# Queries and keys of both layers: one transfer of 128 partitions fills a tile, keys' two parts in one tensor, queries of layer 1 stored by block and map

## The chip, the core and the metric

The kernel runs on one core of one Trainium2 chip. The core has five engines with programs of their own: PE (TensorE, matrix products and transposes), DVE (VectorE), ACT (ScalarE), POOL (GpSimd) and SP (SyncE, which here does nothing but issue transfers). Transfers between the chip's main memory (DRAM) and the on-chip tiles of 128 partitions are carried by 16 DMA engines. SP issues nearly all of them, in the order of its program; a transfer that has to wait for a tile or for data holds up all that stand behind it on SP.

The metric is the device time of one execution in microseconds (us). Durations of single instructions and packets come from one profiled execution.

## What is computed

A trunk of two layers over 2048 tokens of width 1024, in float32. Cut to what matters here:

```python
def even_layer(x, ...):                       # layer 0
    proj = rms_norm(x, norm_g) @ w_in         # queries, keys, values, gates of mixers A and B
    ya = sliding_window_sink_attention(aq, ak, av, a_sinks) * silu(ag)    # 8 query heads, 2 key heads
    yb = chunked_relbias_attention(bq, bk, bv, b_rel) * silu(bg)          # 8 heads
    return x + concatenate([ya, yb]) @ w_out

def odd_layer(x, ...):                        # layer 1
    q, k, v, gate = split(rms_norm(x, norm_g) @ w_in)
    # 8 heads, each with two maps: q1, k1 and q2, k2 of width 64
    a = softmax(q1 @ k1.T / 8) - lam * softmax(q2 @ k2.T / 8)             # keys of the own and earlier chunks
    o = rms_norm(a @ v, subln_g) * (1 - lambda_init)
    return x + (o * silu(gate)) @ w_out
```

## The kernel before

**Two parts of a number.** A product that must be nearly exact is made of two parts of each operand: H, the value rounded to the fast matrix format, and L, the rest. `eH` and `eL` are such a pair for queries and keys. A head has 64 dimensions, which is half of the 128 partitions. A key tile holds H of a head's keys in one half of its partitions and L in the other; a query tile holds the same 64 rows twice, once for each half. So one product over 128 partitions adds query times H and query times L. `qd` holds the H part of the queries twice, `ql` the L part twice.

**Stages.** Four follow each other; a block is 512 tokens, there are four, `b` = 0 to 3.
1. *Projection of layer 0* (`project(0)`): norm, product with the weights, norm and rotation of queries and keys, transposes. `pairs_out` copies each transposed pair of heads into `eH` and `eL` (three buffers each) and stores them to DRAM (L398 and L399), 128 partitions by 512 tokens at a time.
2. *Attention of layer 0* (`mix0`): 16 heads by four blocks, from the last block to the first. `load_q` (L577 to L581) fills `qd` and `ql` (three buffers each) by four transfers of 64 partitions; `load_k` (L587 and L588) fills a key tile by two, H and L. `mks` is the key tile of mixer B (two buffers, 1024 tokens), `mksA` that of mixer A (one for four heads). Output projection and late gates run beside it.
3. *Projection of layer 1* (`project(1)`): two halves of the tokens, in each six groups of weights of 512 columns: values, queries (two groups), keys (two groups), values. Each group is applied to two blocks. Again `pairs_out` stores, in the query groups to `qH` and `qL`, in the key groups to `kH` and `kL`.
4. *Attention of layer 1* (`mix1`): for each head blocks 0 and 1, then block 2 of all heads, then block 3. `load_q` (L926) fills `cqd` and `cql` (two buffers each) by two transfers of 64 partitions each; one row of such a transfer is 2 pieces of 2 KB, one for each map. `load_k` (L1093 and L1094) fills a key tile `ck` of one block and map, H and L apart; there are four buffers for each map. Block `b` needs `b + 1` key tiles for each map; block 3 fills all four buffers, so the next head's keys are loaded as the last row of this head's scores lets go of them. Gates and output projection run beside it.

**What sets the order.** The generators `pace` and `beside` hand out the work of scores, values and side work, and a scheduler then orders each engine's program when the kernel is built.

Queries and keys pass through DRAM: stored by projection, loaded by attention. In DRAM each of `qH`, `qL`, `kH`, `kL` (layer 1), `aqH` ... `bkL` (layer 0) is a tensor of its own, a row of 2048 tokens for each dimension of a head.

Of the kernel before, what the change touches and what calls it, by code (L numbers as in the profile page):

```python
# [11 lines left out]
F32R = mybir.dt.float32r  # L12
# [6 lines left out]
P = 128  # L19
S = 2048  # L20
# [3 lines left out]
BLK = NTB * P  # L24
NB = S // BLK
HD = 64
# [6 lines left out]
def f32(ap):  # L33
    return ap.bitcast(F32)
# [52 lines left out]
class Trunk:  # L87
# [15 lines left out]
    def scratch(self):  # L103
        dram = self.ctx.enter_context(self.tc.tile_pool(name="scr", bufs=1, space=DRAM))

        def d(name, shape):
            return dram.tile(shape, F32, tag=name, name=name)

        self.s0 = {
            "aqH": d("aqH", [4, P, S]), "aqL": d("aqL", [4, P, S]),  # L110
            "akH": d("akH", [1, P, S]), "akL": d("akL", [1, P, S]),
            "av": d("av", [S, 2 * 192]),
            "bqH": d("bqH", [4, P, S]), "bqL": d("bqL", [4, P, S]),
            "bkH": d("bkH", [4, P, S]), "bkL": d("bkL", [4, P, S]),
            "bv": d("bv", [S, 8 * 128]),
            "g": d("g0", [D, S]),
            "woH": d("wo0H", [KT, P, D]), "woL": d("wo0L", [KT, P, D]),
        }
        self.s1 = {
            "qH": d("qH", [8, P, S]), "qL": d("qL", [8, P, S]),  # L120
            "kH": d("kH", [8, P, S]), "kL": d("kL", [8, P, S]),
            "v": d("v", [S, D]),
            "g": d("g1", [D, S]), "o": d("o1", [D, S]),
            "hH": d("hH", [KT, P, S]), "hL": d("hL", [KT, P, S]),
            "woH": d("wo1H", [KT, P, D]), "woL": d("wo1L", [KT, P, D]),
            "wgH": d("wgH", [8, P, KT, P]), "wgL": d("wgL", [8, P, KT, P]),
        }
        self.x1 = d("x1", [S, D])
# [95 lines left out]
    def _project(self, es, layer):  # L224
        nc, tc, a = self.nc, self.tc, self.a
        x = a["x"] if layer == 0 else self.x1
        W = a["ev_w_in"] if layer == 0 else a["od_w_in"]
        s = self.s0 if layer == 0 else self.s1
        n = f"p{layer}"
# [154 lines left out]
        def pairs_out(xs, npair, b, o):  # L384
            for p in range(npair):
                ps = ptr.tile([P, 512], F32, tag="tr", name=n + "trq")
                for j in range(NTB):
                    nc.tensor.transpose(ps[:, j * P:(j + 1) * P], xs[j][:, p * P:(p + 1) * P], self.ident)
                eH = sb.tile([P, 512], F32R, tag="eH", name=n + "eH", bufs=3)
                eL = sb.tile([P, 512], F32R, tag="eL", name=n + "eL", bufs=3)  # L390
                g = self.b_gain
                if not o.get("gain"):
                    nc.scalar.activation(eH, ps, AF.Copy)
                    nc.vector.tensor_tensor(eL, ps, f32(eH), ALU.subtract)
                else:
                    nc.scalar.activation(eH, ps, AF.Copy, scale=g)
                    nc.vector.scalar_tensor_tensor(eL, ps, g, f32(eH), ALU.mult, ALU.subtract)
                nc.sync.dma_start(s[o["dH"]][o["p0"] + p, :, b * BLK:(b + 1) * BLK], f32(eH))  # L398
                nc.sync.dma_start(s[o["dL"]][o["p0"] + p, :, b * BLK:(b + 1) * BLK], f32(eL))  # L399

        def split_weights(W, c0, put, s=s):
            for i in range(2):
# [29 lines left out]
        for half in range(2):  # L432
# [4 lines left out]
            if half == 0 and layer == 0:  # L437
# [3 lines left out]
                h = [hidden(blocks[0], 0, by)]  # L441
            else:
                h = [hidden(blocks[0], 0)]
# [4 lines left out]
            for gi, (kind, c0, width, o) in enumerate(groups):  # L448
# [7 lines left out]
                for bi, b in turns:  # L456
# [21 lines left out]
                    for j in range(NTB):  # L478
                        t = b * NTB + j
                        tok = slice(t * P, (t + 1) * P)  # L480
# [72 lines left out]
    def _mix0(self, es):  # L553
        nc, tc, a, s = self.nc, self.tc, self.a, self.s0
        n = "m"
        pool = lambda nm, bufs, **kw: es.enter_context(tc.tile_pool(name=n + nm, bufs=bufs, **kw))
        sm = pool("sm", 6)
        ld = pool("ld", 2)
# [13 lines left out]
        def load_q(H, L, h, b, res):  # L572
            tok = slice(b * BLK, (b + 1) * BLK)
            e = h % 2
            r = slice(e * HD, (e + 1) * HD)
            qd = ld.tile([P, BLK], F32R, tag="qd", name=n + "qd", bufs=3)
            nc.sync.dma_start(f32(qd[0:HD, :]), s[H][h // 2, r, tok])  # L577
            nc.sync.dma_start(f32(qd[HD:P, :]), s[H][h // 2, r, tok])
            ql = ld.tile([P, BLK], F32R, tag="ql", name=n + "ql", bufs=3)
            nc.sync.dma_start(f32(ql[0:HD, :]), s[L][h // 2, r, tok])  # L580
            nc.sync.dma_start(f32(ql[HD:P, :]), s[L][h // 2, r, tok])  # L581
            res["q"] = (qd, ql)

        def load_k(ks, H, L, p, row, k0, k1):

            r = slice(row * HD, (row + 1) * HD)
            nc.sync.dma_start(f32(ks[0:HD, :k1 - k0]), s[H][p, r, k0:k1])  # L587
            nc.sync.dma_start(f32(ks[HD:P, :k1 - k0]), s[L][p, r, k0:k1])  # L588
            return ks


# [11 lines left out]
        def load_group(b, g):  # L603

            k0, k1 = max(0, b * BLK - P), (b + 1) * BLK
            ks = ld.tile([P, 640], F32R, tag="ksA", name=n + "ksA", bufs=1)
            load_k(ks, "akH", "akL", 0, g, k0, k1)
            vt = ld.tile([P, 5, 192], F32R, tag="vA", name=n + "vA", bufs=1)
            nc.sync.dma_start(
                f32(vt[:, :(k1 - k0) // P, :]),  # L610
                s["av"][k0:k1, g * 192:(g + 1) * 192].rearrange("(t p) c -> p t c", p=P),
            )
            return ks, vt, k0
# [108 lines left out]
        def scores_b(h, b, res):  # L722
            k0, k1 = max(0, (b - 1) * BLK), (b + 1) * BLK
            load_q("bqH", "bqL", h, b, res)
            ks = load_k(ld.tile([P, 1024], F32R, tag="ks", name=n + "ks"), "bkH", "bkL", h // 2, h % 2, k0, k1)
            vt = ld.tile([P, 8, P], F32R, tag="v", name=n + "vB")
            nc.sync.dma_start(
                f32(vt[:, :(k1 - k0) // P, :]),
# [6 lines left out]
            l, r = small("bl", 4), small("br", 4)  # L735
            probs = res["p"] = []
            res.update(v=vt, k0=k0)
            for j in range(NTB):
                t = b * NTB + j
# [5 lines left out]
                m = small("bm", 2)  # L745
# [147 lines left out]
    def _mix1(self, es):  # L893
        nc, tc, a, s = self.nc, self.tc, self.a, self.s1
        n = "c"
        pool = lambda nm, bufs, **kw: es.enter_context(tc.tile_pool(name=n + nm, bufs=bufs, **kw))
        ld = pool("ld", 2)
# [19 lines left out]
            return sm.tile([P, m], F32, tag=tag, name=n + tag)  # L917

        def load_q(h, b):
            tok = slice(b * BLK, (b + 1) * BLK)  # L920
            qd = ld.tile([P, 2, BLK], F32R, tag="qd", name=n + "qd")
            ql = ld.tile([P, 2, BLK], F32R, tag="ql", name=n + "ql")
            for part, q in (("qH", qd), ("qL", ql)):
                both = s[part][h, :, tok].rearrange("(m r) t -> r m t", m=2)
                for o in range(2):
                    nc.sync.dma_start(f32(q[o * HD:(o + 1) * HD]), both)  # L926
            return qd, ql

        def scores(h, b, q, K, res, then):
# [158 lines left out]
        def load_k(h, i, m):  # L1088

            tok = slice(i * BLK, (i + 1) * BLK)  # L1090
            k = kp.tile([P, BLK], F32R, tag=f"k{m}", name=n + f"k{m}")
            r, o = slice(m * HD, (m + 1) * HD), slice((1 - m) * HD, (2 - m) * HD)
            nc.sync.dma_start(f32(k[r, :]), s["kH"][h, r, tok])  # L1093
            self.loaded = nc.sync.dma_start(f32(k[o, :]), s["kL"][h, r, tok]).ins  # L1094
            return k

        def load_v(h, i):
# [266 lines left out]
```

## Time and profile before

| | |
|---|---|
| Time, median of 3 runs (lowest, highest) | 2790.53 us (2790.26, 2792.29) |
| The profiled execution's own time | 2787.34 us |
| Its span, first to last instruction | 2785.4 us |
| PE, DVE, ACT, POOL busy, share of the span | 96%, 65%, 57%, 51% |
| Moved by DMA | 521.64 MB, 187 GB/s on average |
| Stages, by the first and last products of each | layer 0: projection to 560, attention to 1168; layer 1: projection to 1734, attention to the end |

How to read what follows. The page has the busy time of each engine, the DMA queues and the chain of work that ended last. A view by windows gives busy times, the share of time in which the 16 DMA engines are busy, and GB/s for each stretch. A list of DMA issues has one row for each kind of transfer: where to and from, who issued it, how many, KB each, and the median time in us from issue to landing. The view of one tile lists its instructions (count: least, median, greatest duration in ns) and what ended the idle time before them. "DMA x<-y" is a transfer into tile x.

### The profile page before, as it was taken

To read this page: it belongs to the slowest core of one execution; us is meant where nothing else is said; L and a number is where in the kernel's file an instruction comes from. 1 tells how busy PE (TensorE), PEld (TensorE's weight loads), DVE (VectorE), ACT (ScalarE), POOL (GpSimd) and SP (SyncE) were. 2 spreads that over 40 slices of the span, in tenths; PEclk is the share of its full clock that TensorE was granted. 3 is DMA by queue.
4 is the path that set the end of the run, shared out by engine and by line. 5 is a ranking of instruction groups with operands and counts; after the bars stand their busy time and mean duration, and the time that the engine had idled before them with its cause. 6 is when DMAs were issued, how large, how long until landed. Compare 5 with 4: busy or idle time off the path is not lost.

```text
span 2785.4 us, 43642 instructions
## 1 busy us (share of the span) xinstructions
PE 2687.8 (96%) x13384; PEld 2164.0 (78%) x13384; DVE 1814.8 (65%) x4520; ACT 1596.8 (57%) x3975; POOL 1425.9 (51%) x1519
## 2 busy tenths in 40 slices
PE   7999999999899999999999999999999999999999
PEld 6888887888788888788888888777777776676776
DVE  8662286336678776457844783478887787776772
ACT  5443544357777776333243332588887776676771
POOL 3641255235545454325554552467776666667661
PEclk9999999999999999999999999999999999999999
DMA  5674338739777665654386446899877666455542
GB/s 184 213 240 149 110 129 275 239 116 248 221 200 202 192 188 154 200 212 142 130 269 222 131 134 194 250 247 249 213 219 207 198 182 195 125 176 150 165 130 91
DMA packets 354041, 521.64 MB, mean 187 GB/s; under 512 B 42768, under 2 KB 137744, under 8 KB 353808
## 3 DMA queue, kind: packets, MB, share of 16 engines
q1 hardware_dynamic: 349200, 510.47, 61.0%
q10 hardware_dynamic: 4608, 8.39, 0.8%
q8 instruction: 107, 1.75, 0.3%
q14 instruction: 126, 1.03, 0.1%
HBM read 361.70 MB, written 157.02 MB: 186 GB/s over the span
## 4 chain that ended last, share of the span: by engine, by line
PE 68%; DMA 6%; DVE 3%; ACT 3%; issue 2%; POOL 1%; SPq 1%; ACTq 0%; DVEq 0%; POOLq 0%
PE cO L1010 8%; PE p1mm L216 6%; PE p1mm L215 6%; PE p1mm L214 6%; PE cS L951 4%; PE cS L952 4%; PE ctr L1006 4%; PE mom L214 2%; PE mom L215 2%; PE mom L216 2%; PE com L214 2%; PE cG L214 2%; PE com L215 2%; PE cG L215 2%; PE com L216 2%; PE cG L216 2%
## 5 line engine op out<-in xcount | busy, mean ns | idle before, releaser
L958 ACT ACTIVATE cP<-cS,cnm 128x512 f32<-128x512 f32 (+3 forms) x640 | 394.6, 623 | 137.9 <-DVE cnm L955 126.4
L955 DVE TENSOR_REDUCE cnm<-cS 128x1 f32<-128x512 f32 (+3 forms) x640 | 373.4, 600 | 53.8 <-PE cS L952 47.6
L992 POOL TENSOR_TENSOR cP<-cP,cP 128x512 f32<-128x512 f32 (+1 forms) x320 | 356.2, 1140 | 19.2 <-ACT cP L990 18.6
L991 POOL TENSOR_SCALAR cP<-cP,crl,cel 128x512 f32<-128x512 f32 (+3 forms) x288 | 208.8, 737 | 258.4 <-DVE crl L973 111.8
L216 PE MATMUL p1mm<-p1wH,p1hL 128*128 128x512 f32 x768 | 300.5, 392 | 0.0
L214 PE MATMUL p1mm<-p1wH,p1hH 128*128 128x512 f32 x768 | 300.2, 393 | 0.0
L215 PE MATMUL p1mm<-p1wL,p1hH 128*128 128x512 f32 x768 | 299.4, 390 | 0.0
L309 POOL TENSOR_TENSOR p0wL<-p0ws,p0wH 128x512 fp32r<-128x512 f32 (+1 forms) x140 | 169.9, 1240 | 251.0 <-ACT p0wH L307 232.4
L1010 PE MATMUL cO<-cpt,cv 128*128 128x512 f32 (+3 forms) x640 | 286.9, 534 | 5.6 <-DVE cpt L1008 5.6
L951 PE MATMUL cS<-ck,cqd 128*128 128x512 f32 (+3 forms) x640 | 260.6, 411 | 12.5 <-ACT cP L958 11.1
L1008 DVE COPY cpt<-ctr 128x512 f32<-128x512 f32 (+1 forms) x320 | 190.6, 604 | 101.0 <-PE ctr L1006 98.1
L214 PE MATMUL p0mm<-p0wH,p0hH 128*128 128x512 f32 (+1 forms) x640 | 239.1, 377 | 7.4 <-ACT p0vt L497 5.4
L216 PE MATMUL p0mm<-p0wH,p0hL 128*128 128x512 f32 (+1 forms) x640 | 239.3, 374 | 1.3 <-DVE p0hL L335 1.3
L215 PE MATMUL p0mm<-p0wL,p0hH 128*128 128x512 f32 (+1 forms) x640 | 239.5, 374 | 0.0
L952 PE MATMUL cS<-ck,cql 128*128 128x512 f32 (+3 forms) x640 | 233.1, 369 | 1.7 <-DMA cql<-qL 1.7
L1006 PEld LDWEIGHTS ctr<-ident,cP 128*128 128x128 f32 x1088 | 137.3, 141 | 120.0 <-issue 62.6
L309 POOL TENSOR_TENSOR p1wL<-p1ws,p1wH 128x512 fp32r<-128x512 f32 x112 | 154.3, 1402 | 138.8 <-ACT p1wH L307 80.6
L990 ACT ACTIVATE cP<-cP,cc 128x512 f32<-128x512 f32 (+1 forms) x320 | 188.9, 653 | 20.6 <-DVE cc L976 19.6
L1006 PE MATMUL ctr<-ident,cP 128*128 128x128 f32 x1088 | 174.8, 274 | 5.7 <-POOL cP L992 5.7
L216 PEld LDWEIGHTS p1mm<-p1wH,p1hL 128*128 128x128 f32 x768 | 144.2, 188 | 29.4
L215 PEld LDWEIGHTS p1mm<-p1wL,p1hH 128*128 128x128 f32 x768 | 144.3, 188 | 29.0
L214 PEld LDWEIGHTS p1mm<-p1wH,p1hH 128*128 128x128 f32 x768 | 144.3, 188 | 28.5
(320 smaller groups left out, 6937.3 us busy)
## 6 DMA issues: line engine op xcount, KB each, us to landing
p1ws<-in_od_w_in_dram SPq DMA_DIRECT2D x56, 512.0 KB, 3.7
p0ws<-in_ev_w_in_dram SPq DMA_DIRECT2D x48, 512.0 KB, 4.5
ck<-kH SPq DMA_DIRECT2D x144, 128.0 KB, 3.6
ck<-kL SPq DMA_DIRECT2D x144, 128.0 KB, 3.8
cv<-v SPq DMA_DIRECT2D x72, 256.0 KB, 4.4
cqd<-qH SPq DMA_DIRECT2D x64, 256.0 KB, 6.2
cql<-qL SPq DMA_DIRECT2D x64, 256.0 KB, 7.6
cwH<-wgH SPq DMA_DIRECT2D x64, 256.0 KB, 5.3
```

The costliest lines, as they stand in the source:

```text
L214: mm(ps, aH, bH, start=first, stop=False)
L215: mm(ps, aH, bL, start=False, stop=False)
L216: mm(ps, aL, bH, start=False, stop=last)
L309: low.tensor_tensor(l[:, :width], ws[:, k, :width], f32(h[:, :width]), ALU.subtract)
L951: mm(ps, qd[:, m, js], kt[:, :wd], start=True, stop=False)
L952: self.anchor = mm(ps, ql[:, m, js], kt[:, :wd], start=False, stop=True).ins
L955: nc.vector.tensor_reduce(nm[:, m, z:z + 1], ps, AX.X, ALU.max, negate=True)
L958: exp = nc.scalar.activation(chunks[z][:, :wd], ps, AF.Exp, bias=nm[:, m, z:z + 1], accum_out=acc).ins
L991: nc.gpsimd.tensor_scalar(p1, p1, rl[:, 0:1], e1, ALU.mult, ALU.mult)
L992: nc.gpsimd.tensor_tensor(p1, p1, p2, ALU.add)
L1006: nc.tensor.transpose(turned[:, (j - j0) * P:(j - j0 + 1) * P], us[j][kt // 4][:, kk:kk + P], self.ident)
L1010: mm(O[:, j0 * P:], v, T[:, :wd], start=(kt == 0), stop=(kt == nkt - 1), skip_group_check=True)
```

## The change

- The keys' H and L parts become one tensor: `ak`, `bk` and `ck` have a dimension of 2 for the parts. The names `akH`, `akL` and so on remain as views of it for the stores.
- A key load becomes one transfer. Its source is a pattern of 2 parts by 64 dimensions by the tokens; its destination is 128 partitions by the tokens. In layer 1, H now always lies in the lower 64 partitions; before, this depended on the map. The query tile has the same rows in both halves, so the product is the same sum.
- A query load becomes one transfer for each of `qd` and `ql`. Its source is the 64 rows with a leading dimension of 2 and a step of zero, so that each row is read twice; its destination is 128 partitions.
- Queries of layer 1 are stored as `[head, 64, block, map, 512]`: the two maps of a block lie side by side, and a row of a query load is one piece of 4 KB. The store of a pair (128 partitions, two maps of 64) now goes to a pattern of 2 by 64 by 512.

```diff
+        ak, bk, ck = d("ak", [1, 2, P, S]), d("bk", [4, 2, P, S]), d("ck", [8, 2, P, S])
...
-            "akH": d("akH", [1, P, S]), "akL": d("akL", [1, P, S]),
+            "ak": ak, "akH": ak[:, 0], "akL": ak[:, 1],
...
-            "bkH": d("bkH", [4, P, S]), "bkL": d("bkL", [4, P, S]),
+            "bk": bk, "bkH": bk[:, 0], "bkL": bk[:, 1],
...
-            "qH": d("qH", [8, P, S]), "qL": d("qL", [8, P, S]),
-            "kH": d("kH", [8, P, S]), "kL": d("kL", [8, P, S]),
+            "qH": d("qH", [8, HD, NB, 2, BLK]), "qL": d("qL", [8, HD, NB, 2, BLK]),
+            "k": ck, "kH": ck[:, 0], "kL": ck[:, 1],
...
-                nc.sync.dma_start(s[o["dH"]][o["p0"] + p, :, b * BLK:(b + 1) * BLK], f32(eH))
-                nc.sync.dma_start(s[o["dL"]][o["p0"] + p, :, b * BLK:(b + 1) * BLK], f32(eL))
+                for part, t in (o["dH"], eH), (o["dL"], eL):
+                    to = s[part][o["p0"] + p]
+                    by_map = layer == 1 and o["tab"] == "q"
+                    to = to[:, b].rearrange("r m t -> m r t") if by_map else to[:, b * BLK:(b + 1) * BLK]
+                    nc.sync.dma_start(to, f32(t))
...
-            nc.sync.dma_start(f32(qd[0:HD, :]), s[H][h // 2, r, tok])
-            nc.sync.dma_start(f32(qd[HD:P, :]), s[H][h // 2, r, tok])
...
-            nc.sync.dma_start(f32(ql[0:HD, :]), s[L][h // 2, r, tok])
-            nc.sync.dma_start(f32(ql[HD:P, :]), s[L][h // 2, r, tok])
+            for q, part in (qd, H), (ql, L):
+                nc.sync.dma_start(f32(q), s[part][h // 2, r, tok].unsqueeze(0).to_broadcast([2, HD, BLK]))
...
-            nc.sync.dma_start(f32(ks[0:HD, :k1 - k0]), s[H][p, r, k0:k1])
-            nc.sync.dma_start(f32(ks[HD:P, :k1 - k0]), s[L][p, r, k0:k1])
+            nc.sync.dma_start(f32(ks[:, :k1 - k0]), s[K][p, :, r, k0:k1])
...
-                both = s[part][h, :, tok].rearrange("(m r) t -> r m t", m=2)
-                for o in range(2):
-                    nc.sync.dma_start(f32(q[o * HD:(o + 1) * HD]), both)
+                both = s[part][h, :, b].rearrange("r m t -> r (m t)")
+                nc.sync.dma_start(f32(q).rearrange("p m t -> p (m t)"), both.unsqueeze(0).to_broadcast([2, HD, 2 * BLK]))
...
-            r, o = slice(m * HD, (m + 1) * HD), slice((1 - m) * HD, (2 - m) * HD)
-            nc.sync.dma_start(f32(k[r, :]), s["kH"][h, r, tok])
-            self.loaded = nc.sync.dma_start(f32(k[o, :]), s["kL"][h, r, tok]).ins
+            self.loaded = nc.sync.dma_start(f32(k), s["k"][h, :, m * HD:(m + 1) * HD, tok]).ins
```

The next rows are SP's program, where the kernel's transfers stand in the order of issue: line, destination and source, and the destination's pattern, outermost dimension first. First, attention of layer 0, the loads for one head of mixer A and one of mixer B (`mvB` and `mbias` are values and bias of mixer B). Before:

```order
L577 DMA mqd<-aqH 64x512
L578 DMA mqd<-aqH 64x512
L580 DMA mql<-aqL 64x512
L727 DMA mvB<-bv 128x8x128
L581 DMA mql<-aqL 64x512
L587 DMA mks<-bkH 64x1024
L588 DMA mks<-bkL 64x1024
L732 DMA mbias<-in_relb_dram 128x256
```

The same place with the change:

```order
L584 DMA mqd<-aqH 128x1x512
L584 DMA mql<-aqL 128x1x512
L590 DMA mks<-bk 128x1x1024
L729 DMA mvB<-bv 128x8x128
L734 DMA mbias<-in_relb_dram 128x256
```

Six transfers of 64 partitions have become three of 128. The destination has been given a dimension of 1, so that it has as many dimensions as the source, which is 2x64x512 (or 2x64x1024); the source was not folded into one dimension of 128.

Second, projection of layer 1, SP's rows between two loads of weights (`p1ws`), with the change. Before, the stores of queries to `qH` and `qL` had the pattern 128x512:

```order
L303 DMA p1ws<-in_od_w_in_dram 128x2x512 x4
L404 DMA qH<-p1eH 2x64x512 x2
L404 DMA qL<-p1eL 2x64x512 x2
L404 DMA qH<-p1eH 2x64x512
L404 DMA qL<-p1eL 2x64x512
```

Here the destination is the side with an outermost dimension of 2. Number and order of the stores are as before.

Third, attention of layer 1, block 3, from the last key tiles of one head to the next query. Before:

```order
L1093 DMA ck_29834<-kH 64x512
L1094 DMA ck_29834<-kL 64x512
L1172 DMA cxr<-x_83 128x512 x2
L926 DMA cqd<-qH 64x2x512 x2
L1185 DMA out_dram<-cxr 128x512
L926 DMA cql<-qL 64x2x512 x2
```

With the change (`ck` is now also the name of the tensor in DRAM):

```order
L1092 DMA ck_29477<-ck 128x1x512
L926 DMA cqd<-qH 128x1x1024
L1170 DMA cxr<-x_80 128x512
L1098 DMA cv<-v 128x4x128
L1092 DMA ck_29486<-ck 128x1x512
L1170 DMA cxr<-x_80 128x512 x2
L926 DMA cql<-qL 128x1x1024
```

Two transfers have become one for each key tile and for each of `cqd` and `cql`; the last key tile now stands behind `cqd`. On the other engines little moves: with the line numbers taken off, the line-by-line difference of PE's program of some 11,830 rows has about 160 lines, in attention of both layers, where a transpose or a product stands some rows earlier or later.

More of the change, by code (lines that the diff above doesn't have):

```diff
@@ L576, in load_q, with load_k @@
             qd = ld.tile([P, BLK], F32R, tag="qd", name=n + "qd", bufs=3)
-            nc.sync.dma_start(f32(qd[0:HD, :]), s[H][h // 2, r, tok])
-            nc.sync.dma_start(f32(qd[HD:P, :]), s[H][h // 2, r, tok])
             ql = ld.tile([P, BLK], F32R, tag="ql", name=n + "ql", bufs=3)
-            nc.sync.dma_start(f32(ql[0:HD, :]), s[L][h // 2, r, tok])
-            nc.sync.dma_start(f32(ql[HD:P, :]), s[L][h // 2, r, tok])
+            for q, part in (qd, H), (ql, L):
+                nc.sync.dma_start(f32(q), s[part][h // 2, r, tok].unsqueeze(0).to_broadcast([2, HD, BLK]))
             res["q"] = (qd, ql)
-        def load_k(ks, H, L, p, row, k0, k1):
+        def load_k(ks, K, p, row, k0, k1):
             r = slice(row * HD, (row + 1) * HD)
-            nc.sync.dma_start(f32(ks[0:HD, :k1 - k0]), s[H][p, r, k0:k1])
-            nc.sync.dma_start(f32(ks[HD:P, :k1 - k0]), s[L][p, r, k0:k1])
+            nc.sync.dma_start(f32(ks[:, :k1 - k0]), s[K][p, :, r, k0:k1])
             return ks
@@ L606, in load_group @@
             ks = ld.tile([P, 640], F32R, tag="ksA", name=n + "ksA", bufs=1)
-            load_k(ks, "akH", "akL", 0, g, k0, k1)
+            load_k(ks, "ak", 0, g, k0, k1)
             vt = ld.tile([P, 5, 192], F32R, tag="vA", name=n + "vA", bufs=1)
@@ L724, in scores_b @@
             load_q("bqH", "bqL", h, b, res)
-            ks = load_k(ld.tile([P, 1024], F32R, tag="ks", name=n + "ks"), "bkH", "bkL", h // 2, h % 2, k0, k1)
+            ks = load_k(ld.tile([P, 1024], F32R, tag="ks", name=n + "ks"), "bk", h // 2, h % 2, k0, k1)
             vt = ld.tile([P, 8, P], F32R, tag="v", name=n + "vB")
@@ L919, in load_q @@
         def load_q(h, b):
-            tok = slice(b * BLK, (b + 1) * BLK)
             qd = ld.tile([P, 2, BLK], F32R, tag="qd", name=n + "qd")
```

## The prediction

> **What bounds the kernel now.** First the page's first and fourth sections: the busy share of each engine, and the chain of work that ended last; then its transfers.
>
> ```profile
> span 2785.4 us, 43642 instructions
> PE 2687.8 (96%) x13384; PEld 2164.0 (78%) x13384; DVE 1814.8 (65%) x4520; ACT 1596.8 (57%) x3975; POOL 1425.9 (51%) x1519
> PE 68%; DMA 6%; DVE 3%; ACT 3%; issue 2%; POOL 1%; SPq 1%; ACTq 0%; DVEq 0%; POOLq 0%
> DMA packets 354041, 521.64 MB, mean 187 GB/s; under 512 B 42768, under 2 KB 137744, under 8 KB 353808
> q1 hardware_dynamic: 349200, 510.47, 61.0%
> ```
>
> PE is idle for only 98 us of the span and carries 68% of the chain. But SP's queue (q1) keeps all 16 DMA engines busy for 61% of the span, and this is the number to watch: the kernel is bound by PE only while the transfers are spread over all 16. The 61% are 0.61 x 16 x 2785.4 = 27,185 engine-us for 510.47 MB, 18.8 GB/s for each busy engine.
>
> Next the view by windows, cut at the four stages, and two tails that I use below.
>
> ```profile
> core 0: us, PE busy (x) PEld busy (x) DVE busy (x) ACT busy (x) POOL busy (x), PEclk, DMA share, GB/s
> 0.00:560.00 560.00, 531.86 (x2645) 445.57 (x2646) 311.88 (x683) 249.70 (x576) 214.75 (x208) 0.99 0.58 194
> 560.00:1168.00 608.00, 576.20 (x3445) 500.10 (x3444) 397.64 (x1295) 402.36 (x1041) 291.56 (x414) 0.99 0.67 190
> 1168.00:1734.00 566.00, 565.57 (x2689) 472.12 (x2688) 355.28 (x590) 199.38 (x405) 259.71 (x194) 1.00 0.55 179
> 1734.00:2785.00 1051.00, 1014.15 (x4611) 746.26 (x4609) 749.98 (x1952) 745.31 (x1953) 659.86 (x704) 0.99 0.65 187
> 1077.00:1168.00 91.00, 86.48 (x434) 72.74 (x433) 37.84 (x88) 36.81 (x86) 40.70 (x41) 0.98 0.51 166
> 2665.00:2785.00 120.00, 113.43 (x503) 82.98 (x501) 54.23 (x113) 42.90 (x103) 45.69 (x45) 0.99 0.30 101
> ```
>
> The clock is granted nearly in full everywhere. Both attention stages run the DMA engines at about two thirds.
>
> **How many engines carry a transfer.** The list of issues has 2057 transfers; its first and last rows of 76:
>
> ```profile
> p1ws<-in_od_w_in_dram SPq DMA_DIRECT2D x56, 512.0 KB, 3.7
> ...
> mfar<-in_relfar_dram SPq DMA_DIRECT2D x1, 4.0 KB, 2.5
> ```
>
> The page counts 42,768 packets under 512 B. Rows of data account for 9,856 of them: the four loads of the cosine and sine tables (2048 rows of 128 B each), eight loads of gains and lambdas (128 rows of 256 B), and 640 rows of a few bytes. The other 32,912 are 16 x 2057 exactly: every transfer of before ends in 16 small packets, so every one ran on all 16 engines. All of them have an outermost dimension of 64 or 128, the same on both sides.
>
> The change makes 440 transfers whose two sides differ: outermost 2 on one side, 128 on the other. These are 128 + 64 query loads, 40 + 144 key loads and 64 query stores. If an engine is given a run of the outermost index of both sides, there are two runs, and two engines. The order shows that the builder kept the patterns apart (a 1 was added to the 128, the 2x64 was not folded), so nothing that 16 divides is left outermost on that side. No row of before has such a transfer; that it goes by the outermost dimension and not by rows is my judgement from this shape, and the forecast stands on it.
>
> The Trainium skill, "DMA: Bandwidth & Descriptors", section "Why a DMA increments its semaphore by 16 and not by 1", states just this: the number of engines is the largest one up to 16 that divides the slowest dimension of both sides that isn't 1, and on this path the lowest-numbered engines are taken. The same page's "Rules for kernel authors" speaks for the change as well: two transfers to the two partition halves should be one. By the first rule the sum is the forecast's, by the second alone the first rival's; 16 small packets for each transfer agree with both, and no run here shows an outermost 2 yet.
>
> **What one of two engines takes.** Each gets half of a transfer: 64 rows. The trace has a transfer that loads its engines alike: the stores of `hH` and `hL`, 2 MB over 16 engines, which is 64 rows of 2 KB for each. The rows are from the list of issues and SP's timeline.
>
> ```profile
> hH<-p1hH SPq DMA_DIRECT2D x3, 2048.0 KB, 8.8
> hL<-p1hL SPq DMA_DIRECT2D x3, 2048.0 KB, 13.6
> 1209.62 0.37 SPq L341 DMA_DIRECT2D hH<-p1hH  x1
> 1210.45 0.37 SPq L342 DMA_DIRECT2D hL<-p1hL  x1
> ```
>
> `hL` is issued 0.83 us behind `hH` and lands 13.6 + 0.83 - 8.8 = 5.63 us after it. So 131,072 B take an engine 5.63 us in a full queue: 23.3 GB/s, or 88 ns for 2 KB. The alternative is the mean of 18.8 GB/s, which includes rows of 512 B and the crowd of 16 engines; with 14 engines mostly idle I take 23.3 and keep 18.8 for the upper end. For all other traffic on these two engines I take 179 / (16 x 0.55) = 20.3 GB/s, from the window of projection 1.
>
> **The change part by part.** What goes over two engines:
>
> ```profile
> mqd<-aqH SPq DMA_DIRECT2D x64, 128.0 KB, 4.2
> mqd<-bqH SPq DMA_DIRECT2D x64, 128.0 KB, 4.5
> mks<-bkH SPq DMA_DIRECT2D x24, 256.0 KB, 5.7
> mks<-bkH SPq DMA_DIRECT2D x8, 128.0 KB, 3.8
> mksA<-akH SPq DMA_DIRECT2D x6, 160.0 KB, 4.3
> mksA<-akH SPq DMA_DIRECT2D x2, 128.0 KB, 3.5
> qH<-p1eH SPq DMA_DIRECT2D x32, 256.0 KB, 2.8
> ck<-kH SPq DMA_DIRECT2D x144, 128.0 KB, 3.6
> cqd<-qH SPq DMA_DIRECT2D x64, 256.0 KB, 6.2
> cql<-qL SPq DMA_DIRECT2D x64, 256.0 KB, 7.6
> ```
>
> Each H row but the last has its twin for L. The bytes do not change, only how many engines share them.
>
> *Projection 0* keeps its 560 us: its stores keep 128 rows outermost.
>
> *Attention 0.* Queries 4 x 64 x 128 KB and keys 2 x (24 x 256 + 8 x 128 + 6 x 160 + 2 x 128) KB are 49,536 KB = 50.7 MB, 25.4 MB for each of the two engines: 1088 us. The other traffic is 190 x 608 = 115.5 MB less 50.7, a sixteenth of it 4.05 MB: 200 us. Together 1288 us in a stage that lasts 608: the two engines become its bound, and PE's 576 us of work hide behind them. The last query load lands at 1077 (row below); the 91 us after it remain, of which 166 x 91 / 16 / 20.3 = 46 us are counted already. The first loads start 27 us before the stage. 1288 + 91 - 46 - 27 = **1306 us**.
>
> ```profile
> 1069.54 6.97 DMA mql<-bqL
> 2660.38 4.49 DMA ck<-kL
> L577 SPq DMA_DIRECT2D mqd<-aqH x32: 444/450/745, 533.1 to 1060.6; - x32
> L1093 SPq DMA_DIRECT2D ck<-kH x144: 444/540/1903, 1690.8 to 2661.1; - x144
> ```
>
> *Projection 1.* The stores of queries, 64 x 256 KB, are 8.4 MB for each engine: 360 us. They come in 8 of 24 turns (two halves, two of six groups, two blocks), 189 us of PE's time. Three buffers of `eH` and three of `eL` let six stores, 34 us, trail into the key groups of each half. What is left, 360 - 189 - 2 x 34 = 103 us, stalls `pairs_out`, and the weights queue behind the stores. Bounds: nothing, if the other groups take it up, and 171 us, if none does. I take 110: **676 us**.
>
> *Attention 1.* Keys 144 x 256 KB and queries 128 x 256 KB are 71.3 MB, 35.65 MB for each engine: 1530 us. Other traffic 187 x 1051 = 196.5 MB less 71.3, a sixteenth: 385 us. The tail behind the last key load (lands at 2665) 120 us, of which 101 x 120 / 16 / 20.3 = 37 are counted; the first key load is issued 43 us early. A wait is added: in block 3 all four key buffers are full, so the next keys (8 x 5.6 us) can only be asked for as the last row of scores frees them, and stand on SP behind `cqd`; the engines may idle in the rows between. Bounds 0 and 150 us, I take 50. 1530 + 385 + 120 - 37 - 43 + 50 = **2005 us**.
>
> *SP* issues 376 transfers fewer, at 0.45 to 0.59 us each some 200 us. SP's own share of the chain is 1%, 28 us at most, and with the engines' queues full SP waits for buffers anyway: nothing.
>
> The sum: 560 + 1306 + 676 + 2005 = 4547, and 1.9 us that the profiled execution has around its span (2787.3): **4549 us**. The median of the runs shown, 2790.5, is 3 us above that execution; that is nothing here.
>
> **The rivals.**
>
> *All 16 engines after all* (not slower). If the sharing goes by rows, whatever the dimensions, each transfer has 128 rows and lands much as its halves did. What there is to gain is PE's idle time that ended with a query load, from the views of `mSA`, `mSB` and `cS`:
>
> ```profile
>   DMA mql<-aqL: 5.0, 2
>   DMA mql<-bqL: 2.9, 5
>   DMA cql<-qL: 1.7, 2
>   DMA cqd<-qH: 0.6, 1
> ```
>
> That is 10 us, for one issue less ahead of each tile: 2777 us, between 2765 and 2790. For it speaks that every transfer so far had 16 small packets; against it, that none had an outermost 2. It decides if the changed kernel's small packets still number 16 for each transfer.
>
> *Two engines, but others each time* (slower, mildly). The load would stay even at 61%, and only latency would grow: a key load as long as `hH`'s 8.8 us in place of 3.6, a query load some 14 in place of 6 to 8. The chain of before meets a query or key transfer about 13 times; 13 x 6 us, and some 15 us in projection 1 where a store lands later than the three buffers allow: 2880 us. Against it speaks only that a sharing from the lowest engine up is simpler.
>
> **How the numbers follow.** Two fixed engines 0.87, all 16 engines 0.09, changing pairs 0.04. The likeliest gives 4549 us. Its ends: with the tails, the 50 us and the 110 us gone and other traffic at 23.3 GB/s too, about 4190; with queries and keys at 18.8 GB/s, 1088 and 1530 become 1349 and 1896, and the stores cost 86 us more: 5260. I cut this end to 5050, since the `hH` row is nearer, and give 4150 to 5050, 0.92 of the first case; the other cases are the 2 in 10 left out. Slower by over 0.2% (about what a measurement of this kernel tells from no change) 0.91; of the 0.09, 0.06 faster and 0.03 within.
>
> **What would show it.** On two engines: packets under 512 B fall to about 9,856 + 16 x 1241 + 2 x 440 = 30,600 (all 16: 36,750); the DMA share in the attention stages falls to some 0.3 while they last twice as long; a key load takes over 8 us to land, a query load over 14; PE waits for `cql`, `mql` and `ck`; projection 0 keeps its 560 us. It is wrong if a key load lands in about 4 us, or if the engines are two but other traffic overtakes the queue on them.

## The result, and the profile after

The changed kernel takes 4587.8 us, the median of 5 runs (4586.5 to 4589.8), beside 2792.3 us of the kernel before. The ratio is 1.645, with a 95% interval of 1.642 to 1.648: slower, 0.9% above the forecast of 4549 and inside its range. The profiled execution took 4588.1 us.

The page's first, third and fourth sections for the changed kernel (busy time and share of the span; transfers; shares of the chain that ended last):

```profile
span 4586.1 us, 43175 instructions
PE 3003.4 (65%) x13384; PEld 2363.9 (52%) x13384; DVE 1807.2 (39%) x4520; ACT 1601.2 (35%) x3975; POOL 1417.2 (31%) x1519
...
DMA packets 333669, 521.55 MB, mean 114 GB/s; under 512 B 30592, under 2 KB 125568, under 8 KB 333440
...
q1 hardware_dynamic: 328832, 510.42, 33.1%
...
DMA 42%; PE 29%; SPq 8%; issue 4%; DVE 3%; POOL 3%; ACT 1%; POOLq 0%; ACTq 0%; DVEq 0%
```

Look at the small packets first: 30,592 is 9,856 + 16 x 1241 + 2 x 440 to the packet. So each of the 440 transfers ended in two small packets, where the others ended in 16. The bytes are those of before (510.42 MB in q1), but the mean rate fell from 187 to 114 GB/s, and the chain went from 68% PE to 42% DMA. The count of PE's instructions is unchanged.

The windows of the changed kernel, cut at the same stages, with attention 1 cut once more where its last gates end:

```profile
core 0: us, PE busy (x) PEld busy (x) DVE busy (x) ACT busy (x) POOL busy (x), PEclk, DMA share, GB/s
0.00:560.00 560.00, 531.95 (x2652) 445.14 (x2652) 309.51 (x681) 244.59 (x568) 212.33 (x203) 0.99 0.55 184
560.00:1842.00 1282.00, 697.92 (x3440) 588.89 (x3440) 397.45 (x1298) 409.05 (x1049) 291.24 (x418) 0.75 0.28 94
1842.00:2627.00 785.00, 614.64 (x2688) 500.66 (x2685) 350.65 (x590) 191.35 (x403) 256.11 (x194) 0.87 0.37 124
2627.00:4586.00 1959.00, 1158.85 (x4608) 829.19 (x4608) 749.61 (x1952) 756.22 (x1955) 657.48 (x704) 0.77 0.31 102
2627.00:3705.00 1078.00, 586.93 (x2322) 426.19 (x2323) 386.24 (x1131) 412.16 (x1086) 329.86 (x370) 0.74 0.33 109
3705.00:4586.00 881.00, 571.92 (x2288) 403.00 (x2286) 363.37 (x822) 344.06 (x870) 327.62 (x335) 0.80 0.28 94
```

| stage, us | before | forecast | after | forecast missed by |
|---|---|---|---|---|
| projection 0 | 560 | 560 | 560 | 0 |
| attention 0 | 608 | 1306 | 1282 | -24 |
| projection 1 | 566 | 676 | 785 | +109 |
| attention 1 | 1051 | 2005 | 1959 | -46 |

A DMA share of 0.28 reads like an idle machine. It is a mean over 16 engines: two that are always busy are 0.125 of it already. Attention 0's other 69.8 MB (94 x 1282 less 50.7) at 20.3 GB/s on the other 14 engines add 3010 engine-us, or 0.147; together 0.27, and the row has 0.28. The share fell because two engines are full.

A shorter window shows the two engines alone. It lies in the first query turns of projection 1, and SP had issued four stores of queries in the 10 us before it, each of them 5 us of work for two engines:

```profile
1938.00:1956.00 18.00, 8.23 (x28) 6.34 (x28) 8.61 (x11) 1.94 (x5) 7.86 (x6) 0.68 0.13 51
```

A share of 0.13 is 2.1 engines, and 51 GB/s is 25.5 for each of two. Several stores were waiting all this time and two engines worked: the stores share one pair.

PE's five longest waits, from the view of waits of the changed kernel (total us, times, longest us; rows of other engines left out):

```profile
PE cS L951 <- DMA ck<-ck: 292.4, 61, 15.2
PE mSB L620 <- DMA mqd<-bqH: 170.4, 17, 16.7
PE mSB L621 <- DMA mql<-bqL: 115.4, 27, 5.9
PE cG L216 <- DMA cwH<-wgH: 111.6, 9, 20.6
PE cS L951 <- DMA cqd<-qH: 106.9, 6, 24.6
```

Keys and queries, as forecast. `cwH` is a load of gate weights that the change does not touch and that still runs on 16 engines: it pays for standing behind the others. Before, PE waited for it for 6.9 us at most (view of the tile `cG`).

Last, SP's timeline in the window above (start, us, and at the end how many issues the row holds):

```profile
1937.93 5.06 SPq L404 DMA_DIRECT2D qH<-p1eH  x1
1943.04 4.99 SPq L404 DMA_DIRECT2D qL<-p1eL  x1
1948.12 4.96 SPq L404 DMA_DIRECT2D qH<-p1eH  x1
1953.18 3.37 SPq L404 DMA_DIRECT2D qL<-p1eL  x1
1956.64 25.59 SPq L303 DMA_DIRECT2D p1ws<-in_od_w_in_dram  x4
```

The issue of one store holds SP for up to 5 us, where the `hH` and `hL` issues of before took 0.37. The stores follow each other 5.08 us apart, the time in which each of two engines takes its 131,072 B at 25.8 GB/s.

### The profile page after: what moved, and what is told of

Same layout as the page of the kernel before. It is cut to its first block, busy times and chain, and to the rows that moved or that the text cites. A ratio compares the mean times of both kernels' runs of the same rounds, so it can differ in the third digit from the quotient of the medians.

```text
span 4586.1 us, 43175 instructions
## 1 busy us (share of the span) xinstructions
PE 3003.4 (65%) x13384; PEld 2363.9 (52%) x13384; DVE 1807.2 (39%) x4520; ACT 1601.2 (35%) x3975; POOL 1417.2 (31%) x1519
## 2 busy tenths in 40 slices
DMA packets 333669, 521.55 MB, mean 114 GB/s; under 512 B 30592, under 2 KB 125568, under 8 KB 333440
## 3 DMA queue, kind: packets, MB, share of 16 engines
q1 hardware_dynamic: 328832, 510.42, 33.1%
## 4 chain that ended last, share of the span: by engine, by line
DMA 42%; PE 29%; SPq 8%; issue 4%; DVE 3%; POOL 3%; ACT 1%; POOLq 0%; ACTq 0%; DVEq 0%
DMA ck<-ck 11%; DMA mql<-bqL 5%; DMA cql<-qL 5%; DMA cwH<-wgH 4%; PE cO L1010 4%; DMA qL<-p1eL 4%; DMA mbias<-in_relb_dram 3%; DMA mql<-aqL 2%; DMA cwL<-wgL 2%; PE cS L951 2%; PE cS L952 2%; DMA p1ws<-in_od_w_in_dram 2%; PE p1mm L218 2%; PE p1mm L217 2%; PE ctr L1006 2%
## 5 line engine op out<-in xcount | busy, mean ns | idle before, releaser
L951 PE MATMUL cS<-ck,cqd 128*128 128x512 f32 (+3 forms) x640 | 292.6, 460 | 431.3 <-DMA ck<-ck 292.4
L951 PEld LDWEIGHTS cS<-ck,cqd 128*128 128x128 f32 x640 | 136.9, 214 | 488.2 <-issue 412.3
L992 POOL TENSOR_TENSOR cP<-cP,cP 128x512 f32<-128x512 f32 (+1 forms) x320 | 354.9, 1137 | 22.9 <-ACT cP L990 22.5
L217 PE MATMUL p1mm<-p1wL,p1hH 128*128 128x512 f32 x768 | 313.7, 408 | 45.9 <-POOL p1wL L311 45.9
L216 PE MATMUL p1mm<-p1wH,p1hH 128*128 128x512 f32 x768 | 314.8, 412 | 41.3 <-DVE p1xn L371 26.6
L952 PE MATMUL cS<-ck,cql 128*128 128x512 f32 (+3 forms) x640 | 260.5, 409 | 94.1 <-DMA cql<-qL 94.1
L218 PE MATMUL p1mm<-p1wH,p1hL 128*128 128x512 f32 x768 | 312.9, 408 | 0.0
L1010 PE MATMUL cO<-cpt,cv 128*128 128x512 f32 (+3 forms) x640 | 308.2, 569 | 1.7 <-DVE cpt L1008 1.6
L735 POOL TENSOR_SCALAR mbias<-mbias,mfar 128x256 f32<-128x256 f32 x32 | 15.3, 479 | 741.1 <-DMA mbias<-in_relb_dram 741.1
L620 PE MATMUL mSB<-mks,mqd 128*128 128x384 f32 (+2 forms) x240 | 93.0, 388 | 183.5 <-DMA mqd<-bqH 170.4
L952 PEld LDWEIGHTS cS<-ck,cql 128*128 128x128 f32 x640 | 139.5, 218 | 115.0 <-DMA cql<-qL 97.8
```

The lines of the kernel that those rows point to most:

```text
L216: mm(ps, aH, bH, start=first, stop=False)
L217: mm(ps, aH, bL, start=False, stop=False)
L218: mm(ps, aL, bH, start=False, stop=last)
L951: mm(ps, qd[:, m, js], kt[:, :wd], start=True, stop=False)
L952: self.anchor = mm(ps, ql[:, m, js], kt[:, :wd], start=False, stop=True).ins
L992: nc.gpsimd.tensor_tensor(p1, p1, p2, ALU.add)
```

## The experiments

The question was whether the small packets only go along with the loss or whether the two engines are its cause, and which part of the change costs what. Expectations that give "theory" and "rival" mean by the theory the two fixed engines. Kernels measured once are compared with the 2789 to 2791 us that the kernel before took beside them.

**The same transfers, rows outermost.** Still one transfer per tile, one tensor for the keys' parts, queries by block and map, each row read twice. Only the pattern's order differs, and a query store is split by map.

```diff
-                nc.sync.dma_start(f32(q), s[part][h // 2, r, tok].unsqueeze(0).to_broadcast([2, HD, BLK]))
+                nc.sync.dma_start(f32(q), s[part][h // 2, r, tok].unsqueeze(1).to_broadcast([HD, 2, BLK]))
...
-            nc.sync.dma_start(f32(ks[:, :k1 - k0]), s[K][p, :, r, k0:k1])
+            nc.sync.dma_start(f32(ks[:, :k1 - k0]), s[K][p, :, r, k0:k1].rearrange("o r t -> r o t"))
...
-                    to = to[:, b].rearrange("r m t -> m r t") if by_map else to[:, b * BLK:(b + 1) * BLK]
...
+                        for m in range(2):
+                            nc.sync.dma_start(to[:, b, m], f32(t[m * HD:(m + 1) * HD]))
```

> All loads are still one transfer for a tile, rows are still read twice by a step of zero, the keys' parts are still one tensor; but the 64 rows are now the outermost dimension (the two copies, or the two parts, inside it), and the store of queries is split into its two maps. Theory (the outermost dimension sets the number of engines): 16 engines everywhere, 37,776 packets under 512 B, stages as before the change, 2777 us (2755 to 2800). Rival (what costs is reading rows twice in one transfer, or the one tensor for both parts, or the larger transfer): these are all kept, so it stays above 4000 us.

In this kernel rows 2r and 2r+1 of a tile hold what rows r and r+64 held: the order inside the 128 of a sum, the same for queries and keys.

Measured: 2780.1 us (12 runs, 2777.3 to 2788.9) beside 2788.7, ratio 0.997 with an interval of 0.996 to 0.998. Its page on transfers, and two rows from its list of issues (KB each, median us from issue to landing):

```profile
DMA packets 340854, 521.59 MB, mean 187 GB/s; under 512 B 37776, under 2 KB 132752, under 8 KB 340624
...
q1 hardware_dynamic: 336016, 510.45, 57.1%
```

```profile
ck<-ck SPq DMA_DIRECT2D x144, 256.0 KB, 4.2
cql<-qL SPq DMA_DIRECT2D x32, 512.0 KB, 7.3
```

37,776 less 9,856 is 16 x 1745, and there are 1745 transfers. A key load with twice the bytes lands in 4.2 us (its halves took 3.6 and 3.8), the query load in 7.3 (7.6). So none of the rest of the change costs time: not the double reading, not one large transfer, not the tensors' new layout. The outermost 2 does. This is the fastest kernel of the study, 0.3% under before, near the first rival's 2777.

**The stores of queries alone put back on 16 engines** (the third edit of that diff, on the changed kernel).

> The changed kernel with the store of queries alone split into two transfers of 64 outermost rows. Theory (the 219 us that projection 1 grew are these stores on two engines): projection 1 goes back to 566 to 590 us, the rest stays, 4370 to 4400 us in all; 32,512 packets under 512 B. Rival (the weights or the lower clock slow projection 1, whatever the stores): projection 1 stays above 700 us and the time above 4500.

Measured: 4385.5 us, 202 less than the changed kernel. Its windows:

```profile
1843.00:2429.00 586.00, 566.86 (x2683) 472.35 (x2681) 355.66 (x590) 197.75 (x403) 260.65 (x194) 0.99 0.54 167
2429.00:4386.00 1957.00, 1155.36 (x4608) 825.92 (x4608) 750.97 (x1952) 756.55 (x1955) 658.44 (x704) 0.77 0.30 102
```

Projection 1 goes from 785 to 586 us, attention 1 does not move (1957, 1959). Of the 219 us that this stage lost, 199 are the query stores'; 18 of the other 20 are two waits of PE at the end of the stage: 14.5 us for the copy of values `p1v` and 3.5 for the first query load. There SP issues key loads of the next stage, on two engines, ahead of the last stores of keys:

```profile
2375.38 21.66 SPq L1095 DMA_DIRECT2D ck<-ck  x4
```

ACT, which makes `p1v`, stands idle for 30.6 us until a store of `p1eH` behind them has landed.

**Layer 0 alone** (queries and keys of layer 0 as in the change, layer 1 as before).

> The kernel before with the change of layer 0 alone. Theory: attention 0 takes 1282 us in place of 608, every other stage what it took before, 3464 us; the clock granted to TensorE falls to about 0.75 in that stage alone, since it follows PE's waiting. Rival (the low clock of the changed kernel is a cause of its own, which lasts): the later stages run below 0.95 as well, and the time is above 3500 us.

Measured: 3454.6 us. Its windows of attention 0, projection 1, attention 1:

```profile
560.00:1840.00 1280.00, 700.94 (x3452) 592.17 (x3452) 397.75 (x1299) 411.00 (x1053) 292.10 (x418) 0.74 0.28 94
1840.00:2404.00 564.00, 563.88 (x2672) 470.62 (x2673) 353.33 (x590) 197.67 (x402) 260.83 (x194) 1.00 0.55 179
2404.00:3452.00 1048.00, 1010.96 (x4609) 744.35 (x4608) 754.87 (x1952) 745.59 (x1953) 661.62 (x704) 0.99 0.66 187
```

The loss stays in its stage, and so does the low clock.

**Layer 1's keys alone, and layer 1's query loads alone** (each on the kernel before; in the second the query stores are split by map, so that they run on 16).

> The kernel before with the change of the keys of layer 1 alone. Theory (the two engines' queue is the sum of all that passes them): 18.9 MB of keys at 24.4 GB/s, 774 us, and a sixteenth of the other 159 MB, 489 us, with some 50 us of ends: attention 1 takes 1310 to 1350 us in place of 1051, 3050 to 3090 us in all. Rival (774 us of keys fit beside 1051 us of PE, other traffic passes by them): no change, 2780 to 2800 us.

> The kernel before with the change of the queries of layer 1 alone, their store split so that it keeps 64 outermost rows; only the 64 loads of 512 KB go over two engines. By the sum over the whole stage: 33.6 MB, 688 us for each of two engines at 24.4 GB/s, and 502 us of other traffic, 1190 us in place of 1051, 2930 us in all. By the sum over its two parts: up to the last gates 466 us of queries and 293 of other traffic in a part that lasted 516, so 243 us more, and nothing more in blocks 2 and 3 (386 us in 535): 3000 to 3080 us in all. Rival (a row that is read twice by a step of zero is fetched once and costs half): 2790 to 2850 us.

Measured: keys 3306.6 us, queries 3140.2, both above what was expected. Attention 1 in the first; then, of the second, its part with the gates and the rest, and PE's longest wait:

```profile
1749.00:3305.00 1556.00, 1104.53 (x4611) 795.33 (x4609) 749.09 (x1952) 753.31 (x1954) 658.09 (x704) 0.84 0.43 128
```

```profile
1736.00:2548.00 812.00, 550.82 (x2326) 402.14 (x2325) 387.15 (x1131) 408.97 (x1087) 331.63 (x370) 0.83 0.46 144
2548.00:3138.00 590.00, 525.41 (x2286) 379.59 (x2284) 367.05 (x822) 340.68 (x870) 327.28 (x335) 0.94 0.45 139
```

```profile
PE cG L214 <- DMA cwH<-wgH: 92.7, 9, 18.9
```

Keys, by the forecast's rates: 810 us for 18.9 MB and 453 for other traffic outside the tail, with the tail and the early start 1340, and a stage of 1556. Here the bytes on the two engines are only a floor. Queries: 540 us for 48 loads and 282 for other traffic (144 GB/s x 812 us less 25.2 MB, a sixteenth, at 20.3 GB/s), 822 in the part with the gates, which took 812; at the 25.8 GB/s of the stores it is 770. Here the two engines are full. But 55 us are lost in the rest (590, before 535), where by its bytes nothing should be lost.

The single DMA packets of the traces agree. An engine that moves data has a packet under way, so while fewer than two are under way, the two engines are not both at work; packets on other engines hide some of this time, so the count is a lower bound. It is 255 of the 1556 us of the keys, 25 of the 812 us of the queries, and 146 of the 590 behind them. In the part with the gates loads on 16 engines wait too: gate weights stand behind query loads in SP's queue.

**How many engines, at 4 and 8** (the kernel before, with an unused row behind every 16 rows of layer 1's keys in DRAM, so that the rows cannot be folded: key stores have 8 outermost, key loads 4).

```diff
-            "kH": d("kH", [8, P, S]), "kL": d("kL", [8, P, S]),
+            "kH": d("kH", [8, 8, 17, S])[:, :, :16], "kL": d("kL", [8, 8, 17, S])[:, :, :16],
...
-            nc.sync.dma_start(f32(k[r, :]), s["kH"][h, r, tok])
+            nc.sync.dma_start(f32(k[r, :]), s["kH"][h, 4 * m:4 * m + 4, :, tok])
```

> The kernel before, with an unused row after each 16 rows of layer 1's keys in memory, so that a store has 8 outermost rows groups of 16 and a load of 64 partitions has 4; nothing else is changed. Theory (as many engines as the outermost dimension allows): 8 engines for the 64 stores and 4 for the 288 loads, 38,800 packets under 512 B, and a small loss, 2790 to 2870 us. Rival (anything whose outermost dimension isn't a multiple of 16 falls to two engines): 37,840 packets and 3000 us or more. Second rival (sharing by rows): 42,768 packets and no change.

Measured: 38,800 small packets, which is 9,856 + 16 x 1705 + 8 x 64 + 4 x 288 exactly. The outermost dimension sets the engines here too, with no 2 and no double reading in sight. The Trainium skill's rule ("DMA: Bandwidth & Descriptors", "Why a DMA increments its semaphore by 16 and not by 1"), the largest number up to 16 that divides the outermost dimension of both sides, thus agrees with the counts at 2, 4, 8 and 16. The time missed: 3003.1 us is what the first rival gave for two engines, but its 37,840 packets did not come, and the bytes on four engines left little or no loss. Of the 16 key loads among the longest pieces of the chain in this kernel's last 620 us 13 are 9.8 to 12.8 us long, where the four on the chain of before in attention 1 are 3 to 7; two of them (start, us):

```profile
2432.15 7.54 DMA ck<-kH
2439.71 12.57 DMA ck<-kL
```

**A fifth key buffer** (and two fewer for transposed tiles, for room), first on the changed kernel, then on the padded one.

```diff
-        tp = pool("pt", 6)
+        tp = pool("pt", 4)
...
-        kp = pool("kp", 4)
+        kp = pool("kp", 5)
...
-                after, spare = [None, {}], NB - keys(b)
+                after, spare = [None, {}], NB + 1 - keys(b)
```

> The changed kernel with five key buffers for each map in place of four in attention 1, and one more tile of the next head's keys asked for early (two buffers fewer for the transposed weights pay for the space). Bytes and engines stay. Theory (behind the gates attention 1 is bound by keys that can only be asked for as buffers come free, and the two engines idle a fifth of that part): the part from the last gates to the end, 881 us, shortens by 30 to 100 us, 4490 to 4560 us in all, and the part before does not change. Rival (the two engines' bytes bind here too): within 15 us of 4588.

> The padded keys (4 engines for each key load, 3003 us) with five key buffers for each map in place of four and one more tile of the next head's keys asked for early. Bytes and engines stay as in the padded run. Theory (the 212 us there aren't bytes, the engines' work fits in the stage; they are longer landings, which PE meets because keys are asked for only as buffers come free): attention 1 behind the gates, 621 us, shortens by 30 to 86 us, 2915 to 2975 us in all. Rival (four engines are full): within 15 us of 3003.

Measured: 4569.7 us, 18 less than the changed kernel; and 2961.3, 42 less than the padded one. The windows of the padded kernel, and of the same with five buffers:

```profile
1741.00:2378.00 637.00, 543.40 (x2321) 400.88 (x2321) 387.61 (x1130) 408.79 (x1084) 330.64 (x369) 0.90 0.69 188
2378.00:3001.00 623.00, 536.00 (x2289) 383.14 (x2287) 361.46 (x822) 343.65 (x871) 327.21 (x336) 0.93 0.42 129
```

```profile
1750.00:2353.00 603.00, 525.01 (x2313) 388.23 (x2314) 386.42 (x1129) 405.17 (x1080) 329.00 (x366) 0.92 0.71 196
2353.00:2959.00 606.00, 528.07 (x2297) 381.02 (x2295) 363.21 (x824) 344.23 (x876) 329.53 (x339) 0.94 0.44 134
```

The padded kernel gains 34 us ahead of the end of the gates and 17 behind it, so in both parts and not only in the last blocks; behind the gates the theory had asked for 30 at least, and the total lies in its range only with the gain ahead of them. PE's idle time ahead of scores that ended with a load from `kL` falls from 80 us to 33. So waiting for a free key buffer is part of this loss; the other 170 us were not split. In the changed kernel 18 us lie between what the two theories expected, and settle little.

**Layer 1's queries asked for earlier** (on the kernel with its query loads on two engines: at a head's first key tile, not its third), and the same on the kernel with rows outermost.

```diff
-                    if (j, m, z) == (2, 0, 0) and nxt:
+                    if (j, m, z) == (0, 0, 0) and nxt:
```

> The queries of layer 1 alone over two engines (3140 us), with the next query asked for at the first scores of a head in place of the third row's. Bytes and engines stay. Theory (the load of 21 us is asked for too late in the short heads, and what the sum by bytes lacked is this wait): 60 to 130 us faster, 3010 to 3080 us. Rival (two engines are full in the part with gates, which the sum by bytes puts at 759 us of 813): within 20 us of 3140.

> The version with 64 outermost rows everywhere (2780 us), with the next query asked for at the first scores of a head. On 16 engines PE's idle time for queries is a few us: 2770 to 2785 us, no different from that version by more than 0.3%.

Measured: 3198.1 us, 58 more than without, where the theory expected a gain and the rival no change; and 2784.6 (12 runs, ratio 0.998, interval 0.996 to 0.999), no better than rows outermost without it. PE's longest waits in the first, and, for comparison, rows of the same view without the edit:

```profile
PE cS L955 <- DMA cql<-qL: 69.1, 9, 10.7
PE cG L216 <- DMA cwL<-wgL: 66.7, 6, 17.8
PE cG L214 <- DMA cwH<-wgH: 50.5, 6, 14.6
PE com L214 <- DVE cxr L1187: 45.1, 6, 21.3
```

```profile
PE cG L214 <- DMA cwH<-wgH: 92.7, 9, 18.9
PE cS L955 <- DMA cql<-qL: 73.1, 10, 10.7
...
PE com L214 <- DVE cxr L1187: 15.4, 5, 4.1
...
PE cG L216 <- DMA cwL<-wgL: 8.6, 2, 4.4
```

The query parts `cql` are waited for as long as before (69 and 73 us), and other loads are later: gate weights 117 us (101 before), `cxr` (the residual's tile) 45 (15). Asking early in one queue changed who stands behind whom. By the windows, 13 of the 58 us arise in the part with the gates (825 us, before 812) and 45 behind it (635, before 590). In the part with the gates the engines are full by the sum above, so that asking early had nothing to gain there, as the rival said; why the part behind it grew stays open.

**Another order of groups in projection 1** (values, q, k, q, k, values, so that key groups follow each query group).

> The changed kernel with the groups of projection 1 in the order values, queries, keys, queries, keys, values in place of values, queries, queries, keys, keys, values. Bytes and engines stay; after each two turns with stores on two engines come two without. If the stores that trail in the six buffers are taken up by the group behind them, as the prediction had it for 34 us of each half, there are twice as many such places and the groups alone: projection 1, 785 us, loses 60 us or more, 4450 to 4530 us in all. Rival (nothing is taken up, since the trailing stores hold up the weights of the next group in the queue): within 30 us of 785, 4555 to 4620 us.

Measured: 4590.6 us, and projection 1 took 788 us, as with the change (785).

## Why the prediction was right, and where it was not

**The mechanism held at its first step.** The forecast stood on an untested judgement, that the outermost dimension sets the engines. The packets came out at 30,592, and the run with rows outermost shows that this alone makes the difference of some 1800 us. The first rival fell by the condition that it was given (16 small packets for each transfer); the second, changing pairs, would have been near 2880, and the window of 18 us shows stores that wait for one pair.

Of the signs that it gave, the share of the DMA engines (0.28 and 0.31), PE's waits and projection 0 came as written. The list of issues has no landing times for this kernel; on its chain in attention 1 the single key loads take 12.8 to 29.4 us and the loads of `cql` 25.0 to 32.5, where over 8 and over 14 had been forecast:

```profile
2932.54 27.21 DMA cql<-qL
2985.32 29.44 DMA ck<-ck
```

**Attention 0, 1306 forecast, 1282 measured: near, partly by luck.** Taken back from 1282 with the other terms unchanged, the sum gives 25.4 MB in 1064 us, 23.8 GB/s, close to the 23.3 taken. But where two engines work alone they carry 25.5 GB/s and more each. At the stores' 25.8 the bytes take 983 us; with 215 of other traffic, 44 behind the last query load and 27 of early start the sum is 1215, and 67 us are missing. The packets show where: between the first query load and the landing of the last, fewer than two are under way for 68 us. So a rate that was too low made up for waits that the forecast's sum for this stage did not have. Layer 0 alone repeats the stage in 1280 us.

**Projection 1, 676 forecast, 785 measured: the term that was mis-sized.** The step was that "three buffers of `eH` and three of `eL` let six stores, 34 us, trail into the key groups of each half", and with it the 110 us. The stage lost 219 us, and the stores alone cost 199 of them, by the run that put them back on 16 engines: more than the 171 that the forecast had as its upper bound. The buffers were the stall; from the waits in this stage (DVE fills `p1eL`, and waits until a store has left it):

```profile
DVE p1eL L396 <- DMA qL<-p1eL: 151.9, 16, 14.5
```

The window of four query turns, one half's:

```profile
1920.00:2110.00 190.00, 118.64 (x487) 95.07 (x486) 77.63 (x125) 30.09 (x67) 54.94 (x43) 0.79 0.18 63
```

The turns issue 32 stores, 163 us at 5.08 us each; other traffic adds 11 (63 GB/s x 190 us less the stores' 8.4 MB, a sixteenth, at 20.3 GB/s), and some 16 are left, in which the two engines wait. They span 190 us where PE's work for them was 94: two such halves lose 192, which leaves hardly anything that trailed into key groups. The upper bound had set the stores alone against PE's work; the other traffic and the gaps are what it lacked, since the stores themselves were faster than forecast (326 us in place of 360). ACT's timeline shows what stands in the way: the next weights are issued behind the stores, and ACT, which rounds them, had been idle for 21.24 us until they came.

```profile
1973.31 1.15 ACT L309 ACTIVATE p1wH<-p1ws 128x512 fp32r<-128x512 f32 x2 [21.24 <-DMA p1ws<-in_od_w_in_dram]
```

The prediction named this ("the weights queue behind the stores") and then counted the trailing stores as hidden all the same. That other groups did not take them up even with a key group behind each query group fits this; a kernel with its weights asked for ahead of the stores was not tried.

**Attention 1, 2005 forecast, 1959 measured: near, by errors that cancel.** By the starts of the issues, 76 key loads and 48 query loads lie before 3700 us, 68 and 16 behind. The first part has 22.5 MB on each engine, 874 us at 25.8 GB/s, and 223 us of other traffic: 1097 for a part that took 1078, some of it asked for earlier. There the engines are the bound, at a faster rate than the forecast's. The second part has 13.1 MB, 508 us, and 174 of other traffic: 682 in 881. Of the missing 199 us, the tail behind the last key load has its share, which the forecast counted by itself:

```profile
4465.00:4586.00 121.00, 115.11 (x498) 83.98 (x498) 53.40 (x112) 42.00 (x101) 39.43 (x39) 0.97 0.29 96
```

Less the 36 us of other traffic in it, the tail is 85 us, as forecast (83). About 114 us remain for the wait, where the forecast had taken 50, with 150 as the upper bound. By the packets fewer than two are under way for 24 us in the first part, 88 in the second up to the tail, and 74 in the tail, so 88 us is the least that the wait can be. The rate, taken too low, was worth 148 us too many (1530 in place of 1382); the wait was 64 too few, and the other traffic, the tail and the early start together some 38. The fifth buffer shows that free key buffers are some of the wait: 22 us of this part (881 to 859). The rest was not split.

**SP, forecast as nothing.** Fewer issues brought little: the kernel with rows outermost has 312 fewer than before and is 0.3% under it. But issuing was not free: SPq is 8% of the chain. An issue of `cql` to two full engines holds SP for 3.8 us in the median and up to 10, and everything in its program waits along. Much of that is the same time as the full engines and isn't added.

**Do the parts add up?** Alone, layer 0 costs 666 us, layer 1's keys 518, its query loads 349, and its query stores 202 (taken from the changed kernel): 1735. The whole change costs 1796. Of the missing 61, 41 lie in attention 1, where keys and queries cost 867 alone and 908 together on the same two engines.

## What to carry to other kernels

Before two transfers are made one, look at the outermost dimension of both sides as the builder leaves it, and keep there a number that 16 divides: rows outside, copies, parts and maps inside. Count the small packets in the profile against the transfers; they say how many engines each one ran on before any time is understood. Where few engines carry much, the bytes on the fullest engine are a floor, and all that stands behind them in the same queue waits too, whatever number of engines it uses itself.

## What the runs showed of the hardware that was not expected

- **The clock falls in the stages that wait.** The same 13,384 products took PE 2688 us before and 3003 with the change. The granted clock was 0.75, 0.87 and 0.77 in the stages that wait for transfers, and 0.99 in projection 0. With layer 0 alone it was 0.74 in attention 0 and back at 1.00 in the next stage, so the clock goes with the stage. The Trainium skill's page "TensorE: Matmul & The Clock Gate", section "HAM oscillation — how this bites in real kernels", describes waits for transfers that throttle the products after them; the rows agree in direction. Attention 0's 698 us of PE still fit in its 1282; whether the clock costs something where waits and products take turns was not tried.
- **Two engines alone carry 25.5 to 25.8 GB/s each with rows of 2 KB.** So it was for the stores of queries, by the share and rate of the window of 18 us and by the 5.08 us from one store to the next.
- **An issue can wait like a transfer.** SP's rows for `cql` (ns: least, median, most) show issues of up to 9.98 us, against 0.37 us for the 2 MB stores of `hH` over 16 engines.

```profile
L926 SPq DMA_DIRECT2D cql<-qL x32: 479/3756/9977, 2615.9 to 4385.0; - x32
```

- **Long transfers cost beyond their bytes.** On four engines, with the bytes well below what the engines carry, a kernel whose key loads took 10 to 13 us lost 212 us (3003 against 2791); a fifth key buffer gave back 42 of them.
